# Six half units among a pair's head products, seven gathers per layer on the sync queue, and the first unit's sums two steps sooner

## The chip, the cores and the metric

One core of one Trainium2 chip runs the program. The time is device microseconds of one execution; where a profile is shown it is one execution taken by the hardware profiler. Engines: PE does the matmuls, DVE the elementwise work on two operands, ACT the activations and copies, POOL a few small operations, SP only issues DMAs. POOL and ACT can issue DMAs too; each issuing engine has a queue of its own.

## The reference

A trunk of two layers over 256 tokens of width 2048, all in float32:

```
h = rms_norm(x)
q, k, v, uv, gate_logits = split(h @ w_in)        # 1024 + 256 + 256 + 2048 + 4096 columns
a = attention(rope(rms_norm(q)), rope(rms_norm(k)), v, sinks) @ w_attn_branch   # window 128, 16 heads of 64
b = (u * (tril(w_spatial) v_norm + b_spatial)) @ w_sgu_branch                   # uv through gelu; u and v its halves
x = x + (sigmoid(gates)[:2048] * a + sigmoid(gates)[2048:] * b) @ w_out
h2 = rms_norm(x)
x = x + (silu(h2 @ w_gate) * (h2 @ w_up)) @ w_down                             # 5632 columns
```

## The kernel before

**Tiles.** The 256 tokens are two tiles of 128 rows and stay on the chip (xs). All weights are streamed once. The piece they come in is called a *half unit* here: 256 rows by 512 columns of a weight, 512 KB, one DMA on SP's queue (L193). Each piece is split in two: ACT rounds it to a short format (whi, L216) and DVE takes the rest (wlo, L217). The activations are split likewise (uh, ul, a *unit* being 512 of their columns, transposed). Every product is then hi·hi + hi·lo + lo·hi, the three matmuls of L303 to L305, 128x512 each. A half unit is 12 of them.

**Pairs and heads.** Two neighbouring chunks of 512 weight columns, such as two chunks of gates or the gate and up columns of the feed-forward part, make a *pair*. For the first unit of a pair the products are made by a Strassen-like scheme with seven products in place of eight. Six of them, P1, P5, P2, P6, P7, P4, of six matmuls each, make the *head* of the pair; the seventh, P3, and the other half units (tags G and U; X for a chunk without a partner) are its *body*. The scheme needs sums of weights (L204 on DVE) and sums of activations (sums, and their split sh and sl, L446), and it moves partial results while products run:

- after P5, which writes bank a[0], ACT copies a[0] to `kept` (L326) and a[1] to a[0] (L327); P2 goes on in a[0];
- after P6 and after P7 DVE adds a[1] to `kept` (L329); P7 and P4 go on in a[1];
- later the b banks are opened from `kept` (L332).

Each of these must be done before the next product in that bank. So the head is not run in one piece: half units of the plan before are put among its products. There are 49 heads among 1043 entries of the stream.

**Order.** PE's order is written out (the list `entries`). The order of the other engines is set by a scheduler at build time from the data they wait for. Loads are asked for 7 entries ahead, splits 4 ahead (four wsp buffers, so a split waits until PE is done with the one four before), sums 6 ahead. The raw pieces have five buffers, and the four pieces of a head (k11, k12, k21, k22) one each. The smaller work is hung on steps: `after(n, fn)` runs fn n steps later, a step (`tick`) being about one half unit.

**Turning a unit.** Before an activation can be a left operand it is transposed: DVE turns 32x32 blocks into one box (L373, one buffer), and 16 DMAs of 32 KB (L378) gather the box's blocks into tt (or kT for the keys). ACT then makes qT (L695) for the queries, or uh and ul. All gathers are issued by POOL, in order with its small operations, such as rq (L276), the factors of the normalisation of q (L650).

Of the kernel before, what the change touches and what calls it, by code (L numbers as in the profile page):

```python
# [30 lines left out]
B = 32  # L31
W_LOAD = 7
ROUNDS = ((0, 4), (4, 8), (8, 11))
WINO = 0
WINO_NORM = 7, 8, 10, 11, 12, 13
WINO_IN = 6, 7, 8, 12, 13, 14
WINO_MIX = 6, 7, 9, 10, 11, 13
WINO_HID = 7, 8, 17, 18, 19, 20
# [18 lines left out]
def hybrid_trunk(ctx: ExitStack, tc: tile.TileContext, x, mix_norm, w_in, q_norm, k_norm, sinks,  # L57
# [114 lines left out]
    for p in plans:  # L172
        if p.head:
            t = [entries.pop() for _ in range(5)][::-1]
            h = p.head
            entries += [t[0], h[0], t[1], h[1], t[2], h[2], h[3], t[3], h[4], t[4], h[5]]
        entries += p.body

    class Stream:
# [86 lines left out]
    first_cols = const.tile([P, 16], F32, name="first_cols")  # L266
    nc.vector.tensor_copy(first_cols, pf[:, :16])
    neg_half = const.tile([P, 24], F32, name="neg_half")
    nc.gpsimd.memset(neg_half, -0.5)
# [95 lines left out]

    def turn(dst, src):


        box = turned.tile([P, 4, 4, NT, B], F32, tag="box", name=nm("box"))
        iv = src.rearrange("p t (k j c) -> p t k j c", j=4, c=B)  # L370

        def blocks(t):
            nc.vector.transpose(box[:, :, :, t, :].rearrange("p j k r -> p k j r"), iv[:, t])  # L373

        def gather():
            for j in range(4):
                for i in range(4):
                    nc.gpsimd.dma_start(dst[j * B:(j + 1) * B, i], box[i * B:(i + 1) * B, j])  # L378

        blocks(0)  # L380
        after(1, lambda: (blocks(1), gather()))

    def transposed(units, c, src, cols=None, on_pe=False, wino=None, again=False):

# [34 lines left out]
        tt = slot([P, 4, 4, NT, B], name="tt")  # L419
        turn(tt, src)  # L420

# [50 lines left out]
    class Norm:  # L472
# [13 lines left out]
        def unit(self, c, on_pe=False, again=False):  # L486
            transposed(self.units, c, xs[:, :, c * CW:(c + 1) * CW], cols=self.cols[:, 4 * c:4 * c + 4],
                       on_pe=on_pe, again=again,
                       wino=None if c != WINO or on_pe else WINO_IN if self.soon else WINO_NORM)

# [25 lines left out]
    after(7, lambda: norm.finish())  # L516
    after(12, lambda: norm.unit(WINO, again=True))

# [106 lines left out]
    class Attention:  # L625
# [46 lines left out]
        def keys(self, kv):  # L672
            self.kv = kv
            kd = slot([P, NT, NKV, 2, HD], name="kd")
            self.rotate(kv[:, :, :KVW], NKV, self.pl.rope[1], [kd[:, :, :, j, :] for j in range(2)])
            self.kT = slot([P, 4, NKV, NT, B], name="kT")
            after(K_TURN, lambda: turn(self.kT, kd.rearrange("p t n a d -> p t (n a d)")))

        def queries(self, c, q):
            self.rotate(q, NQ // 2, self.pl.rope[0], None)  # L680
            self.qT[c] = slot([P, 4, S], name="qT")
            self.att[c] = slot([P, NT, CW], name="att")
            after(Q_TURN, lambda: self.turn_queries(c, q))
            n = Q_FIRST + (4 * Q_STEP - 8) * c
            for t in range(NT):
                for g in (2 * c, 2 * c + 1):
                    after(n, lambda t=t, g=g: self.scores(t, g))
                    n += Q_STEP
            after(n + 6, lambda: transposed(self.attT, c, self.att[c]))

        def turn_queries(self, c, q):
# [5 lines left out]

            turn(tt, q)
            after(5, lambda: ordered(0))
# [57 lines left out]
    class Spatial:  # L757
# [49 lines left out]
        def u(self, c, ps):  # L807
# [3 lines left out]
            for b in range(2):  # L811
                after(12 + 3 * b, lambda b=b: self.mix(c, b, ut))
            after(18 + 6 * c, lambda: transposed(self.sguT, c, ut))

# [171 lines left out]
```

## Time and profile before

| | |
|---|---|
| median of 3 runs | 2518.38 us (2517.23 to 2518.81) |
| the profiled execution | 2517.02 us |
| its span, first to last instruction | 2515.3 us |
| mean granted clock of PE | 0.994 |
| PE busy | 2477.4 us, 98% |
| DVE busy | 1942.2 us, 77% |
| ACT busy | 1443.6 us, 57% |
| POOL busy | 390.9 us, 16% |
| read from memory | 475.27 MB, 190 GB/s over the span |

The profile is to be read from PE: the idle time of another engine costs nothing unless PE waits for it. In a line of the profile the time stands first, then the engine, the line of the program, the operation and the tiles; brackets name the wait before it and what ended it. The granted clock is the share of full speed that PE was given in a stretch.

### The profile page before, as it was taken

How to read it: one execution, taken by the hardware profiler on the slowest of the kernel's cores; microseconds unless marked ns; L12 is line 12 of the kernel's file. 1: busy time of each engine (PE TensorE's matmuls, PEld its weight loads, DVE VectorE, ACT ScalarE, POOL GpSimd, SP SyncE). 2: the span in 40 equal slices, each digit the busy share in tenths (PEclk: the TensorE clock that was granted, in tenths of full speed). 3: DMA queues.
4: the chain of work that ended last, by engine and by line, in shares of the span. 5: the costliest groups of instructions: out<-in, count | busy, mean ns of one | idle time of the engine just before them, and what ended most of it. 6: DMA issues, size and time to landing. Idle time of an engine off the chain costs nothing. (4 is left out here: it accounts for less than half of the span.)

```text
span 2515.3 us, 31287 instructions
## 1 busy us (share of the span) xinstructions
PE 2477.4 (98%) x11076; PEld 2035.7 (81%) x11076; DVE 1942.2 (77%) x2279; ACT 1443.6 (57%) x1808; POOL 390.9 (16%) x751
## 2 busy tenths in 40 slices
PE   9899999999999999999999999999999999999999
PEld 7678888788888888888887788887888888888887
DVE  6788766688877778777888986767878777877786
ACT  5566545566655565455666665445756555655564
POOL 3401212131110011002114012122311101110110
PEclk9999999999999999999999999999999999999999
DMA  8555657567575666566667556675766666665754
GB/s 294 172 158 177 194 176 236 188 193 232 179 234 175 220 199 220 182 208 211 209 181 237 153 158 211 201 216 172 229 194 219 199 201 204 208 208 186 223 185 151
DMA packets 272078, 502.54 MB, mean 200 GB/s; under 512 B 26224, under 2 KB 28880, under 8 KB 271920
## 3 DMA queue, kind: packets, MB, share of 16 engines
q1 hardware_dynamic: 248720, 476.90, 60.1%
q0 software_dynamic: 22880, 23.37, 3.1%
q8 instruction: 87, 1.43, 0.2%
q14 instruction: 71, 0.58, 0.1%
q10 hardware_dynamic: 320, 0.27, 0.0%
HBM read 475.27 MB, written 2.10 MB: 190 GB/s over the span
## 5 line engine op out<-in xcount | busy, mean ns | idle before, releaser
L217 DVE TENSOR_TENSOR wlo<-raw,whi 128x1024 fp32r<-128x1024 f32 (+1 forms) x1045 | 1271.4, 1219 | 528.3 <-ACT whi L216 519.2
L216 ACT ACTIVATE whi<-raw 128x1024 fp32r<-128x1024 f32 (+1 forms) x1045 | 1104.0, 1058 | 973.5 <-PE acc L305 823.7
L303 PE MATMUL acc<-whi,uh 128*128 128x512 f32 x3094 | 1213.4, 392 | 16.1 <-ACT acc L327 10.2
L304 PE MATMUL acc<-wlo,uh 128*128 128x512 f32 x3094 | 1207.5, 390 | 2.3 <-DVE wlo L217 2.3
L305 PE MATMUL acc<-whi,ul 128*128 128x512 f32 x3094 | 1207.3, 390 | 0.0
L303 PEld LDWEIGHTS acc<-whi,uh 128*128 128x128 f32 x3094 | 582.6, 188 | 140.3 <-ACT acc L327 12.6
L304 PEld LDWEIGHTS acc<-wlo,uh 128*128 128x128 f32 x3094 | 582.8, 188 | 124.1 <-DVE wlo L217 4.8
L305 PEld LDWEIGHTS acc<-whi,ul 128*128 128x128 f32 x3094 | 582.5, 188 | 122.7 <-DVE ul L405 0.2
L378 POOL DMA_DIRECT2D tt<-box x672 | 329.7, 498 | 1727.8 <-DVE box L373 655.9
L204 DVE TENSOR_TENSOR raw<-raw,raw 128x1024 f32<-128x1024 f32 x196 | 238.9, 1219 | 0.5
L303 PE MATMUL acc<-whi,sh 128*128 128x512 f32 x392 | 158.8, 405 | 5.9 <-DVE kept L329 5.8
L305 PE MATMUL acc<-whi,sl 128*128 128x512 f32 x392 | 154.4, 394 | 4.3 <-DVE sl L446 4.3
L304 PE MATMUL acc<-wlo,sh 128*128 128x512 f32 x392 | 154.3, 394 | 0.0
L303 PEld LDWEIGHTS acc<-whi,sh 128*128 128x128 f32 x392 | 74.5, 190 | 32.9 <-issue 12.4
L305 PEld LDWEIGHTS acc<-whi,sl 128*128 128x128 f32 x392 | 74.7, 191 | 20.7 <-DVE sl L446 4.7
L304 PEld LDWEIGHTS acc<-wlo,sh 128*128 128x128 f32 x392 | 74.7, 190 | 14.0
L329 DVE TENSOR_TENSOR kept<-acc,kept 128x512 f32<-128x512 f32 x98 | 66.8, 682 | 3.9 <-PE acc L305 3.9
L332 ACT ACTIVATE acc<-kept 128x512 f32<-128x512 f32 x98 | 56.4, 587 | 6.4 <-DVE kept L329 6.3
L837 DVE SCALAR_TENSOR_TENSOR xs<-acc,xs 128x512 f32<-128x512 f32 (+1 forms) x66 | 42.6, 667 | 7.8 <-PE acc L305 7.8
L925 ACT ACTIVATE hid<-acc,rhalf 128x512 f32<-128x512 f32 x44 | 30.4, 690 | 19.2 <-PE acc L305 19.1
L326 ACT ACTIVATE kept<-acc 128x512 f32<-128x512 f32 x49 | 29.3, 597 | 15.1 <-PE acc L305 15.1
L728 ACT ACTIVATE pr<-pr,negm 128x128 f32<-128x128 f32 (+1 forms) x64 | 28.2, 443 | 7.8 <-DVE negm L721 7.7
(136 smaller groups left out, 899.9 us busy)
## 6 DMA issues: line engine op xcount, KB each, us to landing
raw<-in_w_in_dram SPq DMA_DIRECT2D x239, 512.0 KB, 4.4
raw<-in_w_up_dram SPq DMA_DIRECT2D x176, 512.0 KB, 4.7
raw<-in_w_gate_dram SPq DMA_DIRECT2D x176, 512.0 KB, 4.6
raw<-in_w_down_dram SPq DMA_DIRECT2D x176, 512.0 KB, 4.8
raw<-in_w_out_dram SPq DMA_DIRECT2D x64, 512.0 KB, 4.7
tt<-box POOLq DMA_DIRECT2D x672, 32.0 KB, 4.2
raw<-in_w_attn_branch_dram SPq DMA_DIRECT2D x32, 512.0 KB, 4.5
raw<-in_w_sgu_branch_dram SPq DMA_DIRECT2D x32, 512.0 KB, 4.2
```

Of the source, the lines that this page charges most:

```text
L204: self.last = nc.vector.tensor_tensor(out=self.raws[d], in0=self.raws[x], in1=self.raws[y], op=ALU.subtract)
L216: nc.scalar.activation(hi[:, i, :], raw[:, i, :], AF.Copy)
L217: self.last = nc.vector.tensor_tensor(out=lo[:, i, :], in0=raw[:, i, :], in1=hi[:, i, :].bitcast(F32), op=ALU.subtract)
L303: nc.tensor.matmul(ps, a, hi[:, kk, :], start=first and kk == 0, stop=False, skip_group_check=True)
L304: nc.tensor.matmul(ps, a, lo[:, kk, :], start=False, stop=False, skip_group_check=True)
L305: nc.tensor.matmul(ps, b, hi[:, kk, :], start=False, stop=kk == 1, skip_group_check=True)
L326: nc.scalar.activation(p.kept[:, 1, :], a[0], AF.Copy)
L329: nc.vector.tensor_tensor(out=p.kept[:, int(tag == "P7"), :], in0=a[1], in1=p.kept[:, 1, :], op=ALU.add)
L332: nc.scalar.activation(ps, p.kept[:, t, :], AF.Copy)
L378: nc.gpsimd.dma_start(dst[j * B:(j + 1) * B, i], box[i * B:(i + 1) * B, j])
L837: nc.vector.scalar_tensor_tensor(out=xs[:, t, sl], in0=sums[t][:, i * w:(i + 1) * w], scalar=scale, in1=xs[:, t, sl], op0=ALU.mult, op1=AL ...
L925: nc.scalar.activation(th, g[t], AF.Tanh, scale=norm.rh[t])
```

## The change

Four edits.

1. **Order of a head.** Before, five half units of the plan ahead stand around and among the head's products: t0 P1 t1 P5 t2 P2 P6 t3 P7 t4 P4. Now it is n, the smaller of six and the number of entries in that plan's body. With six: t0 P1 t1 P5 t2 t3 P2 P6 t4 P7 t5 P4. With four, where the plan ahead is a chunk of a branch product with four half units: t0 P1 t1 P5 P2 P6 t2 P7 t3, and P4 comes after the first entry of the pair's own body. 45 heads get six, four get four: in each layer the pair of gate chunks 5 and 6 and the first pair of the output projection (mix).
2. **Queue.** `turn` takes the queue of the gather. The gathers of kT, of the two chunks of q, of the two of the attention's result and of the two of the gating unit go to SP, 7 per layer, 14 in all and 224 DMAs. The other 30 stay on POOL.
3. **First unit's sums.** For the first unit of layer 0, made a second time from a gather (`again`), the steps are 6 to 11 in place of 7, 8 and 10 to 13.
4. **Its start.** That gather is hung on step 10 in place of 12.

```diff
@@ -34,6 +34,7 @@
 WINO = 0
 WINO_NORM = 7, 8, 10, 11, 12, 13
 WINO_IN = 6, 7, 8, 12, 13, 14
+WINO_FIRST = 6, 7, 8, 9, 10, 11
 WINO_MIX = 6, 7, 9, 10, 11, 13
 WINO_HID = 7, 8, 17, 18, 19, 20
 W_SPLIT = 4
@@ -171,10 +172,15 @@
     entries = []
     for p in plans:
         if p.head:
-            t = [entries.pop() for _ in range(5)][::-1]
-            h = p.head
-            entries += [t[0], h[0], t[1], h[1], t[2], h[2], h[3], t[3], h[4], t[4], h[5]]
+            h, n = p.head, min(6, len(ahead.body))
+            t = [entries.pop() for _ in range(n)][::-1]
+            entries += [t[0], h[0], t[1], h[1]] + t[2:n - 2] + [h[2], h[3], t[n - 2], h[4], t[n - 1]]
+            if n == 6:
+                entries.append(h[5])
+            else:
+                p.body.insert(1, h[5])
         entries += p.body
+        ahead = p
     class Stream:
@@ -265,6 +271,7 @@
     nc.tensor.transpose(pf[:, :16], first_rows, ident[:16, :16])
     first_cols = const.tile([P, 16], F32, name="first_cols")
     nc.vector.tensor_copy(first_cols, pf[:, :16])
+
     neg_half = const.tile([P, 24], F32, name="neg_half")
     nc.gpsimd.memset(neg_half, -0.5)
@@ -363,7 +370,7 @@
         while p.left:
             step()
-    def turn(dst, src):
+    def turn(dst, src, queue):
         box = turned.tile([P, 4, 4, NT, B], F32, tag="box", name=nm("box"))
@@ -375,12 +382,12 @@
         def gather():
             for j in range(4):
                 for i in range(4):
-                    nc.gpsimd.dma_start(dst[j * B:(j + 1) * B, i], box[i * B:(i + 1) * B, j])
+                    queue.dma_start(dst[j * B:(j + 1) * B, i], box[i * B:(i + 1) * B, j])
         blocks(0)
         after(1, lambda: (blocks(1), gather()))
-    def transposed(units, c, src, cols=None, on_pe=False, wino=None, again=False):
+    def transposed(units, c, src, cols=None, on_pe=False, wino=None, again=False, queue=None):
@@ -417,7 +424,7 @@
             return
         tt = slot([P, 4, 4, NT, B], name="tt")
-        turn(tt, src)
+        turn(tt, src, queue or nc.gpsimd)
         def blocks_of(k0):
             return lambda k, step: tt[:, :, k0 + k:k0 + k + step].rearrange("p i k t r -> p (k t) i r")
@@ -486,7 +493,8 @@
         def unit(self, c, on_pe=False, again=False):
             transposed(self.units, c, xs[:, :, c * CW:(c + 1) * CW], cols=self.cols[:, 4 * c:4 * c + 4],
                        on_pe=on_pe, again=again,
-                       wino=None if c != WINO or on_pe else WINO_IN if self.soon else WINO_NORM)
+                       wino=None if c != WINO or on_pe else WINO_FIRST if again else WINO_IN if self.soon else
+                       WINO_NORM)
         def finish(self):
             self.r, self.rh, self.rr = [], [], []
@@ -514,7 +522,7 @@
     for c in range(NCH):
         after(3 + c, lambda c=c: norm.squares(c))
     after(7, lambda: norm.finish())
-    after(12, lambda: norm.unit(WINO, again=True))
+    after(10, lambda: norm.unit(WINO, again=True))
     mask = const.tile([P, S], F32, name="mask")
     nc.gpsimd.memset(mask, 0.0)
@@ -674,7 +682,7 @@
             kd = slot([P, NT, NKV, 2, HD], name="kd")
             self.rotate(kv[:, :, :KVW], NKV, self.pl.rope[1], [kd[:, :, :, j, :] for j in range(2)])
             self.kT = slot([P, 4, NKV, NT, B], name="kT")
-            after(K_TURN, lambda: turn(self.kT, kd.rearrange("p t n a d -> p t (n a d)")))
+            after(K_TURN, lambda: turn(self.kT, kd.rearrange("p t n a d -> p t (n a d)"), nc.sync))
         def queries(self, c, q):
             self.rotate(q, NQ // 2, self.pl.rope[0], None)
@@ -686,7 +694,7 @@
                 for g in (2 * c, 2 * c + 1):
                     after(n, lambda t=t, g=g: self.scores(t, g))
                     n += Q_STEP
-            after(n + 6, lambda: transposed(self.attT, c, self.att[c]))
+            after(n + 6, lambda: transposed(self.attT, c, self.att[c], queue=nc.sync))
         def turn_queries(self, c, q):
             tt = slot([P, 4, 4, NT, B], name="tt")
@@ -695,7 +703,7 @@
                 nc.scalar.activation(self.qT[c][:, k:k + 2].rearrange("p k (t i r) -> p (k t) i r", t=NT, r=B),
                                      tt[:, :, k:k + 2].rearrange("p i k t r -> p (k t) i r"), AF.Copy)
-            turn(tt, q)
+            turn(tt, q, nc.sync)
             after(5, lambda: ordered(0))
             after(6, lambda: ordered(2))
@@ -810,7 +818,7 @@
                 after(1 + t, lambda t=t: self.gelu(ut, t))
             for b in range(2):
                 after(12 + 3 * b, lambda b=b: self.mix(c, b, ut))
-            after(18 + 6 * c, lambda: transposed(self.sguT, c, ut))
+            after(18 + 6 * c, lambda: transposed(self.sguT, c, ut, queue=nc.sync))
         def mix(self, c, b, ut):
             pg = ps_at.tile([P, 2, NT, P], F32, tag="at", name=nm("psg"))
```

What the edits do to the rows of ACT at the pair of gate chunks 5 and 6 in layer 0, before. whi_3224 is the split for P5, 3246 for t2, 3259 for P2, 3279 for P6, 3293 for t3, 3311 for P7:

```order
L216 ACTIVATE whi_3224<-raw_3127 128x1024
L216 ACTIVATE whi_3246<-raw_3185 128x1024
L216 ACTIVATE whi_3259<-raw_3204 128x1024
L216 ACTIVATE whi_3279<-raw_3127 128x1024
L326 ACTIVATE kept_3290<-acc_3251 128x512
L216 ACTIVATE whi_3293<-raw_3244 128x1024
L327 ACTIVATE acc_3251<-acc_3252 128x512
L216 ACTIVATE whi_3311<-raw_3129 128x1024
L216 ACTIVATE whi_3324<-raw_3277 128x1024
```

The same place now; whi_3246 is for P5, 3265 for P2, 3279 for P6, 3298 for t2, 3311 for P7. The lines are some six to eight further down in the changed file (L216 is L222, L326 is L333, L327 is L334):

```order
L222 ACTIVATE whi_3246<-raw_3145 128x1024
L222 ACTIVATE whi_3265<-raw_3203 128x1024
L222 ACTIVATE whi_3279<-raw_3145 128x1024
L222 ACTIVATE whi_3298<-raw_3244 128x1024
L333 ACTIVATE kept_3308<-acc_3269 128x512
L222 ACTIVATE whi_3311<-raw_3147 128x1024
L334 ACTIVATE acc_3269<-acc_3270 128x512
```

The copies L326 and L327, which wait for P5, had a split between them and half unit t2 stood between P5 and P2 on PE; the split between them is there now too, and P2 is the product next to P5.

ACT at the first head of layer 1, before (qT is the transposed first chunk of q; whi_11236 is the split for P2, 11256 for P6, 11270 for t3, 11289 for P7):

```order
L216 ACTIVATE whi_11236<-raw_11181 128x1024
L216 ACTIVATE whi_11256<-raw_11079 128x1024
L216 ACTIVATE whi_11270<-raw_11220 128x1024
L216 ACTIVATE whi_11289<-raw_11081 128x1024
L695 ACTIVATE qT_10994<-tt_11127 128x512
L326 ACTIVATE kept_11267<-acc_11227 128x512
L695 ACTIVATE qT_10994<-tt_11127 128x512
L327 ACTIVATE acc_11227<-acc_11228 128x512
```

And now (whi_11236 is the split for P2, 11251 for P6, 11270 for t4, 11289 for P7):

```order
L222 ACTIVATE whi_11236<-raw_11181 128x1024
L333 ACTIVATE kept_11246<-acc_11206 128x512
L334 ACTIVATE acc_11206<-acc_11207 128x512
L222 ACTIVATE whi_11251<-raw_11060 128x1024
L222 ACTIVATE whi_11270<-raw_11216 128x1024
L222 ACTIVATE whi_11289<-raw_11062 128x1024
L703 ACTIVATE qT_10994<-tt_11128 128x512 x2
L222 ACTIVATE whi_11305<-raw_11249 128x1024
```

The two copies have moved from behind qT to three splits ahead of it.

SP in the first head of layer 0 now; tt_833 is the gather of the first chunk of q, which stood on POOL:

```order
L199 DMA raw_978<-in_w_in_dram 128x2x512
L199 DMA raw_1012<-in_w_in_dram 128x2x512
L199 DMA raw_1091<-in_w_in_dram 128x2x512
L385 DMA tt_833<-box_834 32x256 x16
L199 DMA raw_1104<-in_w_in_dram 128x2x512
L199 DMA raw_1117<-in_w_in_dram 128x2x512
L199 DMA raw_1146<-in_w_in_dram 128x2x512
```

The 16 DMAs of a gather stand among the loads of the half units and are issued when the box is turned, with the loads behind them.

## The prediction

> **What bounds the kernel now.** I read the page's totals first, then PE's list of waits, then the stretches around the waits with the busy time of every engine, then single instructions there. The lines of the page for the engines, and PE's waits (engine, line, what it waited for: us in total, times, longest):
>
> ```profile
> PE 2477.4 (98%) x11076; PEld 2035.7 (81%) x11076; DVE 1942.2 (77%) x2279; ACT 1443.6 (57%) x1808; POOL 390.9 (16%) x751
> ...
> PE acc L303 <- ACT acc L327: 10.2, 7, 4.5
> PE acc L303 <- DVE kept L329: 6.8, 10, 2.6
> PE acc L305 <- DVE sl L446: 4.3, 1, 4.3
> PE psc L711 <- ACT qT L695: 3.6, 1, 3.6
> PE acc L303 <- ACT gate L869: 2.7, 1, 2.7
> PE acc L304 <- DVE wlo L217: 2.3, 5, 0.6
> PE acc L303 <- ACT q L869: 1.8, 1, 1.8
> ```
>
> PE bounds it: of the 2515.3 us span 2477.4 are busy and only about 34 us are waits that these rows name. No matmul is removed, so nothing but these waits, and the clock behind them, can be won. The rows are a map: L327 (the copy that P2 needs), L329 (the sum that P7 and P4 need), sl (the first unit's sums) and qT are what the edits touch; the gate drain is not touched.
>
> The stretches in which they lie (us, then busy time of PE, PEld, DVE, ACT, POOL, then the granted clock):
>
> ```profile
> core 0: us, PE busy (x) PEld busy (x) DVE busy (x) ACT busy (x) POOL busy (x), PEclk, DMA share, GB/s
> 89.90:119.70 29.80, 19.61 (x71) 14.67 (x69) 26.77 (x34) 14.32 (x24) 11.01 (x18) 0.83 0.35 100
> 468.70:477.50 8.80, 4.31 (x13) 3.01 (x13) 4.98 (x6) 5.38 (x8) 0.00 (x0) 0.82 0.53 179
> 1354.50:1368.10 13.60, 9.98 (x41) 7.19 (x39) 13.12 (x15) 6.96 (x9) 2.89 (x2) 0.87 0.51 158
> 168.00:181.00 13.00, 10.42 (x41) 8.73 (x40) 12.05 (x28) 5.31 (x13) 1.00 (x1) 0.74 0.71 203
> ```
>
> These are the first head of layer 0, the first mix pair, the first head of layer 1 and the second head of layer 0. In three of the four it is DVE that is nearly full (26.77 of 29.80, 13.12 of 13.60, 12.05 of 13.00): there PE waits for a backlog, and a wait removed at one product may return at the next. The mix pair is another kind: ACT and DVE are half idle, a single chain on ACT is late.
>
> What a wait costs beyond itself shows in PE's instructions behind it (start, length, in brackets the wait before it):
>
> ```profile
> 473.62 0.50 PE L303 MATMUL acc<-whi,uh 128*128 128x512 f32 x1 [4.49 <-ACT acc L327]
> ...
> 474.51 0.63 PE L303 MATMUL acc<-whi,uh 128*128 128x512 f32 x1
> 474.93 0.63 PE L304 MATMUL acc<-wlo,uh 128*128 128x512 f32 x1
> ...
> 172.91 0.47 PE L303 MATMUL acc<-whi,sh 128*128 128x512 f32 x1 [2.58 <-DVE kept L329]
> ...
> 92.06 0.50 PE L303 MATMUL acc<-whi,uh 128*128 128x512 f32 x1 [1.77 <-ACT q L869]
> 92.40 0.39 PE L304 MATMUL acc<-wlo,uh 128*128 128x512 f32 x1
> 92.63 0.39 PE L305 MATMUL acc<-whi,ul 128*128 128x512 f32 x1
> ```
>
> Starts are 0.23 us apart at full clock (92.40 to 92.63) and 0.42 after the long idle (474.51 to 474.93). The matmuls behind the 2.58 and the 4.49 us waits ran so for six or seven instructions, some 1.3 us lost; those behind the 1.77 us wait did not. Restarting costs about 0.3 us besides (0.34 in place of 0.23 to the second matmul, and the overlap of some 0.16 lost). So a wait of w costs w + 0.3, and w + 1.6 once it is long.
>
> **The change part by part.** The profiled execution took 2517.02 us; the median of the three runs is 2518.38, 1.36 higher. I sum differences and take them off the median.
>
> *First unit's sums earlier, q's gather off POOL (first head).* Three of the rows above stand here: q 1.8, sl 4.3, qT 3.6. The stretch of 29.80 us holds 10.2 us of PE idle; with some 16 slow matmuls (3.2) and four restarts (1.2) that is 14.5 us lost. DVE and POOL there:
>
> ```profile
> 89.89 1.22 DVE L650 TENSOR_TENSOR q<-q,rq 128x1024 f32<-128x1024 f32 x1
> 95.06 1.23 DVE L661 TENSOR_TENSOR q<-q,ca 128x1024 f32<-128x1024 f32 x1
> 97.58 1.30 DVE L373 STREAM_TRANSPOSE box<-q 128x512 f32<-128x512 f32 x2
> 99.91 1.21 DVE L446 TENSOR_TENSOR sl<-sums,sh 128x1024 fp32r<-128x1024 f32 x1
> 122.13 0.66 DVE L329 TENSOR_TENSOR kept<-acc,kept 128x512 f32<-128x512 f32 x1
> ...
> 71.36 3.93 POOL L378 DMA_DIRECT2D kT<-box  x8
> 82.81 2.93 POOL L276 TENSOR_TENSOR rq<-ssq,neg_half 128x16 f32<-128x16 f32 x1
> ```
>
> POOL gathered kT from 71.36 to 82.8, and rq, which the rotation of q needs, came behind it. So the rotation sat on DVE at 89.89 to 97.5, just where sl and the head's sums fall due; sl came at 99.91 and P5 stood 4.28 us. With kT's gather on SP, rq is ready before 83, and the rotation lies in the half units before the head, where DVE still had gaps. In the new order sl also stands directly behind P1's split, two splits ahead of P5's. The DVE list from q's product to P7's sum (89.89 to 122.79, 33 us, 3 of them idle) loses the rotation (four operations, 5.0), sl (1.2), and, now behind the sum of P6 or P7, one operation and the two transposes of the next q (2.4): 8.6 less. P7's sum ends near 114 in place of 122.8. What stays late: qT by about 1.3 (its gather still follows the rotation), P2 by about 1.6 (the order puts P7's split ahead of its copy), P7 by about 2.6. With restarts that is some 7 of the 14.5: gain **7.5**. If DVE stays as full as now only the sl wait less a returned wait is won: 2. If P7 does not wait: 12.
>
> *Six half units (45 heads).* The copy that P2 needs has one half unit more. In the first head of layer 1 it is behind qT today:
>
> ```profile
> 1356.31 0.63 ACT L695 ACTIVATE qT<-tt 128x512 f32<-128x512 f32 x1 [0.27 <-DMA tt<-box]
> ...
> 1357.84 0.59 ACT L327 ACTIVATE acc<-acc 128x512 f32<-128x512 f32 x1
> ...
> 1358.48 0.80 PE L303 MATMUL acc<-whi,uh 128*128 128x512 f32 x1 [3.59 <-ACT acc L327]
> ```
>
> The new order has both copies three splits ahead of qT. The wait of 3.59 and 1.6 behind it are 5.2; DVE is full at 13.12 of 13.60, so I give 1.5 back at the sums: gain **3.7** (2 to 5.2). In the second head the 2.58 us wait for L329 costs 4.2 with its clock; the sum waits for a backlog of 12.05 in 13.00, and P7 comes one half unit (2.7 us) later: gain **3.6** (1 to 4.2). The small ones, L327 (five waits, 2.1 together) and L329 (nine, 4.2 together): the extra half unit hides the copies wholly, the sums only partly, since P7 still follows P6 by one half unit: **3.0** (0.7 to 4). The other heads never waited, and win nothing.
>
> *Four half units (the pair of gate chunks 5 and 6, the first mix pair; both layers).* Here the plan before has four half units only, and by the new order no half unit stands between P5 and P2. What P2 then waits for is visible at the second head, where the same three instructions follow P5's end:
>
> ```profile
> 160.07 0.60 ACT L326 ACTIVATE kept<-acc 128x512 f32<-128x512 f32 x1 [0.25 <-PE acc L305]
> 160.57 1.05 ACT L216 ACTIVATE whi<-raw 128x1024 fp32r<-128x1024 f32 x1
> 161.52 0.59 ACT L327 ACTIVATE acc<-acc 128x512 f32<-128x512 f32 x1
> ```
>
> From 160.07 to 162.11, with the signal 2.1 to 2.2 us, and today a half unit of 2.7 us covers it. That cover is gone. Queued behind the copy on ACT are only the splits of the next half units, four ahead of PE. Price: 2.15, restart 0.3, and the slow clock, which 1.77 did not bring and 2.58 did; I take half of 1.6: **3.3** each, bounds 2.1 and 4.1. Three of the four heads pay it whole, the one before layer 1's mix pair perhaps 0.6 more, since its P1 bank is drained by two gate activations. In layer 0's mix pair the 4.5 us wait is already there, and the same chain (a split, uh, two gate drains, two copies) starts from P5's end instead: 0. Sum **−10.5** (−6.9 to −13).
>
> [...]
>
> *Gathers on SP.* Seven gathers per layer, 14 in all, of 16 DMAs of 32 KB. Nothing is copied more or less; the queue that weights come through is held.
>
> ```profile
> L217 DVE TENSOR_TENSOR wlo<-raw,whi 128x1024 fp32r<-128x1024 f32 (+1 forms) x1045 | 1271.4, 1219 | 528.3 <-ACT whi L216 519.2
> L216 ACT ACTIVATE whi<-raw 128x1024 fp32r<-128x1024 f32 (+1 forms) x1045 | 1104.0, 1058 | 973.5 <-PE acc L305 823.7
> L378 POOL DMA_DIRECT2D tt<-box x672 | 329.7, 498 | 1727.8 <-DVE box L373 655.9
> ...
> L193 SPq DMA_DIRECT2D raw<-in_w_in_dram x239: 367/368/753, 3.6 to 1683.2; - x120
> ...
> raw<-in_w_in_dram SPq DMA_DIRECT2D x239, 512.0 KB, 4.4
> ...
> tt<-box POOLq DMA_DIRECT2D x672, 32.0 KB, 4.2
> ```
>
> At 0.367 us an issue 16 take 5.9 us; if the ninth waits for the first to land (on POOL kT's gather was broken so, 11.4 us with its gaps), 8.8 to 11.4. Cover: five buffers freed every 2.72 us, less a split of 1.2 and a landing of 4.4, leave 8 us until a split is late, and the splits run four ahead, 3 × 2.72 − 1.06 − 1.22 = 5.9 until PE is. 13.9 in all, more than 11.4: cost **0**. Without that cover each gather costs its excess.
>
> Sum: 7.5 + 3.7 + 3.6 + 3.0 − 10.5 = 7.3 gained. **2518.4 − 7.3 = 2511.1.**
>
> **The rivals.** *Fuller gains.* The clock keeps full speed at 2.15 us, and P7 no longer waits in the first two heads: the first head gains 12, the next two 5.2 and 4.2, the small ones 3, and the four heads cost 8: 16.4 gained at most, 13.9 with the first head at 9.5: 2504.5. For it: the 1.77 us wait. Against: DVE's shares above.
>
> *DVE takes the gains back.* The window rows say DVE bounds three of the four stretches, and no DVE instruction is removed there but only moved a few half units. First head 2 to 3, first head of layer 1 2, second head 1, small ones 2, together 7 to 8, against 8 to 10.5 paid at the four heads: no change, 2520 (2516 to 2522).
>
> *Slower: SP is held.* One gather holds SP past 13.9 us when it waits for its box's second transpose and then lands as slowly as kT's on POOL; the loads behind it come late, and PE waits for whi. At 16 us each 14 gathers would cost 14 × 2 = 28, less 7: 2539. It decides from 13.9 us on. Against: the order puts the loads next to each gather five to ten half units ahead of their splits.
> [...]
>
> *It doesn't do what it says*: the new order is not six half units at the four heads, as counted above.
>
> **How the numbers follow.** Forecast 0.46, fuller gains 0.20, DVE takes it back 0.24, slower 0.10. A difference under 0.2% (5.0 us) cannot be told from none. The forecast's own range is 2506.5 to 2515.5; its slower end, about a fifth of its chance, lies inside the 0.2%. Faster: 0.37 + 0.20 = 0.57; same: 0.24 + 0.09 = 0.33; slower 0.10. The range takes in the fuller gains down to 2503.5 and the third case up to 2520.
>
> **What would show it.** Right: PE's wait for sl gone; the L327 row with four waits of 2.1 to 4.5 us, all at heads with P2 directly behind P5, and about 1.6 at the first head; the L329 row near 3 to 5 us; P5 without a wait at the first head and the wait for qT near 1.3; no wait of PE or ACT for raw; PE busy shorter by the slow matmuls. Wrong: PE waits for whi or wlo behind a gather, a wait for qT as long as before, or L329 waits as large as the L327 waits that went.

## The result

The changed kernel takes 2503.10 us (median of 4 runs, 2502.16 to 2503.58), the kernel before 2517.81 (4 runs, 2515.98 to 2518.81). The ratio is 0.9942, 95% interval 0.9925 to 0.9959: 14.7 us faster. Forecast was 2511.1, 7.3 less, with a range that ended at 2503.5. The direction was right, the gain twice as large, and the time lies outside the range by 0.4 us, near the rival of fuller gains (2504.5). One execution in the whole record, of bare49_long below, took 4319.45 us at a mean granted clock of 0.553; no number here uses it.

The page of the changed kernel, the line of the engines, and PE's list of waits, with the same columns as before. L310 is the former L303, L311 is L304, L334 is L327, L336 is L329, L877 is L869, L703 is L695, L719 is L711:

```profile
PE 2470.9 (99%) x11076; PEld 2030.7 (81%) x11076; DVE 1950.7 (78%) x2279; ACT 1441.6 (58%) x1808; POOL 288.3 (12%) x527
...
PE acc L310 <- ACT acc L334: 12.2, 5, 4.5
PE acc L310 <- ACT gate L877: 4.0, 1, 4.0
PE acc L310 <- DVE mv L801: 1.7, 1, 1.7
...
PE psc L719 <- ACT qT L703: 1.7, 1, 1.7
PE acc L311 <- DVE wlo L223: 1.6, 3, 0.8
...
PE acc L310 <- DVE kept L336: 0.7, 1, 0.7
```

Two readings. The row for the copy (L334) has grown from 10.2 to 12.2 us, although 45 heads were given more room: five waits are left, three of 2.12, one of 4.5 and one of 1.3 at the first head. The row for DVE's sum fell from ten waits and 6.8 us to one of 0.7, and the rows for sl and for q's drain are gone.

The table sums, at each place, the time between the starts of neighbouring matmuls above 0.227 us, their median in the traces of before and after. It holds the wait, the restart and the slow clock, and so can be added up.

| place | before | after | gained | forecast |
|---|---|---|---|---|
| first head of layer 0 | 14.4 | 5.9 | 8.4 | 7.5 |
| second head | 4.9 | 2.3 | 2.7 | 3.6 |
| first head of layer 1 | 5.9 | 1.0 | 4.9 | 3.7 |
| 11 small waits of 0.2 to 0.5 us at other heads | 7.7 | 0 | 7.7 | 3.0 |
| the four heads with four half units, and the gate wait beside the last | 12.2 | 21.2 | −9.1 | −10.5 |
| all else | 17.2 | 18.6 | −1.4 | 0 |
| sum | 62.2 | 49.0 | 13.2 | 7.3 |

The span went from 2515.3 to 2500.5, by 14.8; the sum leaves out the time between the small matmuls of the attention and the transposes.

### The profile page after: what moved, and what is told of

Same layout as the page of the kernel before. It is cut to its first block, busy times and chain, and to the rows that moved or that the text cites. A ratio compares the mean times of both kernels' runs of the same rounds, so it can differ in the third digit from the quotient of the medians.

```text
span 2500.5 us, 31319 instructions
## 1 busy us (share of the span) xinstructions
PE 2470.9 (99%) x11076; PEld 2030.7 (81%) x11076; DVE 1950.7 (78%) x2279; ACT 1441.6 (58%) x1808; POOL 288.3 (12%) x527
## 5 line engine op out<-in xcount | busy, mean ns | idle before, releaser
L222 ACT ACTIVATE whi<-raw 128x1024 fp32r<-128x1024 f32 (+1 forms) x1045 | 1103.6, 1058 | 955.0 <-PE acc L312 767.7
L310 PE MATMUL acc<-whi,uh 128*128 128x512 f32 x3094 | 1213.0, 392 | 18.6 <-ACT acc L334 12.2
L311 PE MATMUL acc<-wlo,uh 128*128 128x512 f32 x3094 | 1207.4, 390 | 1.2 <-DVE wlo L223 0.8
L310 PEld LDWEIGHTS acc<-whi,uh 128*128 128x128 f32 x3094 | 582.3, 188 | 141.7 <-ACT acc L334 14.1
L311 PEld LDWEIGHTS acc<-wlo,uh 128*128 128x128 f32 x3094 | 582.5, 188 | 124.2 <-DVE wlo L223 4.4
L385 POOL DMA_DIRECT2D tt<-box x480 | 236.1, 499 | 1732.9 <-DVE box L380 608.2
L310 PE MATMUL acc<-whi,sh 128*128 128x512 f32 x392 | 158.0, 403 | 2.3 <-DVE mv L801 1.7
L311 PE MATMUL acc<-wlo,sh 128*128 128x512 f32 x392 | 153.6, 392 | 0.8 <-DVE wlo L223 0.8
L310 PEld LDWEIGHTS acc<-whi,sh 128*128 128x128 f32 x392 | 74.0, 189 | 29.3 <-issue 10.7
L311 PEld LDWEIGHTS acc<-wlo,sh 128*128 128x128 f32 x392 | 74.1, 189 | 14.8 <-DVE wlo L223 1.1
L336 DVE TENSOR_TENSOR kept<-acc,kept 128x512 f32<-128x512 f32 x98 | 66.9, 683 | 0.5 <-PE acc L312 0.5
L934 DVE SCALAR_TENSOR_TENSOR hid<-hid,acc 128x512 f32<-128x512 f32 x44 | 29.8, 684 | 9.3 <-ACT hid L933 9.3
L333 ACT ACTIVATE kept<-acc 128x512 f32<-128x512 f32 x49 | 29.2, 595 | 13.2 <-PE acc L312 13.2
```

The costliest lines, as they stand in the source:

```text
L222: nc.scalar.activation(hi[:, i, :], raw[:, i, :], AF.Copy)
L310: nc.tensor.matmul(ps, a, hi[:, kk, :], start=first and kk == 0, stop=False, skip_group_check=True)
L311: nc.tensor.matmul(ps, a, lo[:, kk, :], start=False, stop=False, skip_group_check=True)
L336: nc.vector.tensor_tensor(out=p.kept[:, int(tag == "P7"), :], in0=a[1], in1=p.kept[:, 1, :], op=ALU.add)
L385: queue.dma_start(dst[j * B:(j + 1) * B, i], box[i * B:(i + 1) * B, j])
L934: nc.vector.scalar_tensor_tensor(out=th, in0=th, scalar=1.0, in1=g[t], op0=ALU.add, op1=ALU.mult)
```

## Experiments

"Lost" below is the sum that the table uses, for one place. The experiments ran on three chips, which ran the kernel before in 2515.3 to 2515.8 us (medians), so they are compared by their ratios to it.

**five_at_four.** The four heads get the old order back, with the fifth half unit from the plan further ahead:

```diff
-            h, n = p.head, min(6, len(ahead.body))
+            h, n = p.head, 6 if len(ahead.body) >= 6 else 5
```

(with P4 always behind the last of them).

> The change, with the old order of five half units at the four heads whose plan ahead has four. Theory A (the four heads cost what the profile of the change shows there: two new waits of 2.12 us at P2 worth 2.7 each, and at the mix pair of layer 1 9.4 in place of 5.8, 9.1 in all; the rest of the change is independent of them): the waits of 2.12 us go, the gate wait is 2.7 again, and the time is 2503.1 - 9.1 = 2494. Rival B (the new order there pays by itself, since P4 behind G2 frees the last half unit, and what I read as price is the drain of the gates, late in any order): 2501 to 2504. By the price in the prediction (10.5): 2492.6.

Measured 2492.94 us, ratio 0.9912 (0.9898 to 0.9927). The change's own ratio is 0.9942, so the four heads cost about 0.3%, 7.5 us; by the spans, 2500.5 and 2493.5, 7.0. The three waits of 2.12 us are gone, and at the mix pair of layer 1 2.8 are lost in place of 9.4. The price was real, as theory A has it. It came out smaller than 9.1, since a wait that theory A did not know appeared at 299 us:

```profile
289.12 1.06 ACT L218 ACTIVATE whi<-raw 128x1024 fp32r<-128x1024 f32 x1 [2.58 <-DMA tt<-box]
...
297.04 1.16 ACT L399 ACTIVATE uh<-tt 128x512 fp32r<-128x512 f32 x2 [5.87 <-DMA tt<-box]
...
299.61 1.06 ACT L218 ACTIVATE whi<-raw 128x1024 fp32r<-128x1024 f32 x1 [0.84 <-DMA raw<-in_w_in_dram]
300.96 1.06 ACT L218 ACTIVATE whi<-raw 128x1024 fp32r<-128x1024 f32 x1 [0.30 <-DMA raw<-in_w_in_dram]
302.23 1.06 ACT L218 ACTIVATE whi<-raw 128x1024 fp32r<-128x1024 f32 x1 [0.21 <-DMA raw<-in_w_in_dram]
...
275.71 3.71 SPq L195 DMA_DIRECT2D raw<-in_w_in_dram  x7
279.52 16.10 SPq L381 DMA_DIRECT2D tt<-box  x16
295.72 1.55 SPq L195 DMA_DIRECT2D raw<-in_w_in_dram  x3
```

These are ACT's and SP's instructions (start, length). The second gather of the gating unit holds SP for 16.1 us, the loads behind it go out at 295.7, and the splits wait for raw. PE stood 0.75 us for whi and 0.77 for wlo.

**six_alone.** Only the order of the 45 heads, on the kernel before.

```diff
-            t = [entries.pop() for _ in range(5)][::-1]
+            n = 6 if len(ahead.body) >= 6 else 5
+            t = [entries.pop() for _ in range(n)][::-1]
```

> The kernel before with six half units at 45 heads and the old five at the other four; gathers on POOL and the first unit's sums as before. Theory A (the extra half unit alone removes the waits at the small heads, 6.9, at the first head of layer 1, 4.9, and at the second head of layer 0, 2.7): 14.5 less than before plus what P2's share of the first head gives, so 2502 to 2504. Rival (the two heads among queries and keys gained because the gathers left POOL): only the small heads, 2517.8 - 6.9 = 2511.

Measured 2501.99, ratio 0.9952 (0.9935 to 0.9968): 12 us less by the ratio, 13.5 by the medians. (The expectation took the small waits at 6.9 us; counted over all of them they are 7.7.) All eleven small waits are gone, so the rival is false; the second head loses 2.3 (4.9 before), the first head of layer 1 2.2 (5.9). The first head of layer 0 loses 14.6, as before. So the order explains, without the queue, all the gain but that of the first head.

**queue_sums, sums_alone, queue_alone.** The kernel before with the gathers on SP and the earlier sums, with the sums alone (`after(10, ...)` and WINO_FIRST), and with the queue alone (`queue.dma_start` with nc.sync for the 14 gathers).

> The kernel before with the gathers on SP and the first unit's sums two steps sooner, the order of the heads as before. Theory A: the first head of layer 0 gains its 8.4 by these two and nothing else moves, 2517.8 - 8.4 = 2509.4; the wait for sl is gone, that of 3.6 at the first head of layer 1 and the 4.5 at the first mix pair stay. Rival (the first head's gain needs the half unit between P5 and P2 too): 3 to 5 less than before, 2513 to 2515. Rival (holding SP costs): slower than 2517.8, with waits of PE for whi.

> The kernel before with only the first unit's sums two steps sooner. If the late sl is late because its step is late: its wait of 4.28 us goes, with its clock some 6 us, 2512, and the wait for qT stays 3.6 or grows. If it is late because DVE is full there (the rotation of q sits at the same place, since rq waits for POOL): the wait moves to the next product, and the time is within 2 us of before, 2516 to 2518.

> The kernel before with only the 14 gathers on SP. sums_alone won 2.3 and the two together 5.4 by medians (11 in their profiles). Theory (the rotation of q, early since rq no longer stands behind kT's gather, is what empties DVE there): first head 14.4 to about 7, 5 to 8 less than before, ratio 0.9975. Rival (sl is late by its step, whatever DVE does): the wait of 4.3 for sl stays, 2 to 3 less than before, 0.999.

| | median | ratio | lost at the first head | waits of PE there |
|---|---|---|---|---|
| sums_alone | 2513.17 | 0.9992 (0.9983 to 1.0001) | 11.7 | q 1.8, qT 5.9 |
| queue_alone | 2513.21 | 0.9991 (0.9981 to 1.0000) | 9.3 | q 1.8, qT 2.6, one more of 1.0 |
| queue_sums | 2510.04 | 0.9976 (0.9966 to 0.9986) | 4.4 | qT 1.4, P2's copy 1.8, P7's sum 0.9 |

(The kernel before loses 14.4 there.) The earlier step alone takes away the wait for sl, and the wait for qT grows from 3.6 to 5.9: DVE is as full as it was, and the wait has moved to the next product, as its second branch has it (2.0 less by the ratio). The queue alone takes away the same wait for sl, though its step is late: its rival expected 4.3 to stay, and it falls. How, DVE's instructions in queue_alone show:

```profile
80.14 1.23 DVE L653 TENSOR_TENSOR q<-q,rq 128x1024 f32<-128x1024 f32 x1 [0.42 <-POOL rq L278]
...
96.36 1.22 DVE L448 TENSOR_TENSOR sl<-sums,sh 128x1024 fp32r<-128x1024 f32 x1
```

The product of q with rq starts at 80.14 and not at 89.89, and sl comes at 96.36 and not at 99.91. That is the step of the prediction on rq behind kT's gather. With both, the first head's gain is there without the extra half unit, so the rival that needs it is false by the profile: 10 us less are lost at that place. By the medians the two give 5.4 (3.5 to 8.6 by the interval); the profiled execution, 2506.1, is the fastest of nine that reach to 2512.5. queue_alone gains less than its theory says: 5.1 at the first head in place of 7, of which the first head of layer 1 takes 1.4 back (7.3 lost, 5.9 before).

**sgu_pool and kt_only.** five_at_four with the gating unit's gathers back on POOL, and with all but kT's back.

```diff
-            after(18 + 6 * c, lambda: transposed(self.sguT, c, ut, queue=nc.sync))
+            after(18 + 6 * c, lambda: transposed(self.sguT, c, ut))
```

> five_at_four with the gathers of the gating unit (4 of the 14) back on POOL. In five_at_four SP was held for 16.1 and 15.3 us by the second of two such gathers, beyond the 13.9 us of cover, and PE waited for whi and wlo there (0.75 and 0.77 us at 300, 0.75 at 1542, 4.7 us with the clock behind them). If those waits are the loads held behind the gather, they go and the time is 3 to 4.5 less than five_at_four, a ratio to before of about 0.9896; if they come from elsewhere, nothing changes (0.9912).

> sgu_pool with the gathers of q and of the attention's result back on POOL too: only kT's gather is on SP. Theory A (the queue matters at the first head only because rq stood behind kT's gather on POOL): the first head costs some 5.5 as in five_at_four, ratio to before about 0.9896 as in sgu_pool. Rival (what helps is that the gathers from SP land in 1.9 us and not 4.2): the wait for qT grows by 2 to 3 us in the first head and the queries of layer 1 get one; 3 to 5 us slower than sgu_pool, about 0.991.

sgu_pool took 2496.75, ratio 0.9924 (0.9912 to 0.9936): no gain. The waits for held loads did go, as expected, but the gate wait at the mix pair of layer 1 rose from 2.5 to 5.9 us. ACT there, then POOL's issues of the gather that uh waits for; in the second block the same issues in five_at_four:

```profile
1685.55 1.06 ACT L218 ACTIVATE whi<-raw 128x1024 fp32r<-128x1024 f32 x1 [0.31 <-PE acc L308]
1690.94 1.15 ACT L399 ACTIVATE uh<-tt 128x512 fp32r<-128x512 f32 x2 [4.33 <-DMA tt<-box]
1692.00 1.24 ACT L873 ACTIVATE gate<-acc,rhalf 128x512 f32<-128x512 f32 x2
...
1677.33 3.42 POOL L381 DMA_DIRECT2D tt<-box  x7 [10.09 <-ACT whi L218]
1683.31 4.40 POOL L381 DMA_DIRECT2D tt<-box  x9 [2.56 <-issue]
```

```profile
1681.65 7.81 POOL L381 DMA_DIRECT2D tt<-box  x16 [9.70 <-ACT whi L218]
```

The gate drain that frees PE's bank stands behind uh, and uh waits for its gather. That gather is on POOL in all kernels. In sgu_pool its 16 issues were broken by a pause of 2.56 us and took 10.4 us in place of 7.8, which is most of the 3.4 us by which the wait grew. What makes POOL pause is not shown.

kt_only took 2507.84, ratio 0.9967 (0.9955 to 0.9979), 11 us slower than sgu_pool. Theory A (only kT's gather matters) is false: with q's gathers on POOL the first head loses 8.8 in place of 5.8, the first head of layer 1 3.8 in place of 1.2, and some 4.4 more go in the two stretches behind it. That is more than twice what the rival expected, and its cause, the landing, explains a small part only. In the page's table of DMAs one DMA of a gather lands in 4.2 us (median; 4.1 in kt_only) when POOL issues it and in 1.9 when SP does, but SP takes longer to issue the 16: for the first chunk of q 10.0 us in sgu_pool, where POOL took 7.9 in kt_only. From the end of the second transposition to the last landing the gather of the first chunk of q takes 11.3 us in sgu_pool and 11.5 in kt_only; in layer 1 11.9 and 14.1, with a pause among POOL's issues there:

```profile
1332.59 3.49 POOL L381 DMA_DIRECT2D tt<-box  x7 [1.08 <-PE acc L308]
1338.56 4.55 POOL L381 DMA_DIRECT2D tt<-box  x9 [2.48 <-issue]
```

What else differs is the order of ACT. In sgu_pool qT starts within 0.2 us of the landing. In kt_only it stands behind splits and starts 1.2 us after it at the first head and 3.7 us after it in layer 1 (landed 1346.13, started 1349.85). So moving the gathers changed the order that the scheduler made, and the 11 us are not the price of the queue alone; how they part was not tested.

**late_unit and late_unit_pool.** In five_at_four and sgu_pool, the unit of the third chunk for the mix pair is made four steps later, so that its uh does not stand ahead of the gate drain and the two copies on ACT.

```diff
-            after(6, lambda: parts(0, 2, blocks_of(0)))
-            after(7, done)
+            after(at[0], lambda: parts(0, 2, blocks_of(0)))
+            after(at[1], done)
...
+                                                                   at=(10, 11) if j in (2,) else (6, 7)))
```

> five_at_four, with the unit of the third chunk for the mix pair (uh, ul) made four steps later. Theory: the 4.5 us wait at the first mix pair (before, after and in every kernel so far) and the gate wait at layer 1's are one thing: on ACT the gate drain and the two copies stand behind that unit's uh, which waits for its gather. Both waits go (7.3 and 2.8 us with their clock): 10 less than five_at_four, a ratio to before of 0.987. Rival (the copies wait for a buffer or for P5 as such): the wait stays between 2 and 4.5, ratio 0.990 to 0.991.

> late_unit with the gating unit's gathers back on POOL. In sgu_pool this removed the waits for held loads (3.7 and 1.0) and the gate wait grew from 2.5 to 5.9 with a slow clock, because uh waited longer for its gather with the drain behind it. With the drain no longer behind uh the first remains and the second is gone: 4 to 4.7 less than late_unit, ratio 0.985. If moving those gathers costs by itself (POOL is held for others), no gain over late_unit.

late_unit took 2483.11, ratio 0.9874 (0.9859 to 0.9889), where 0.987 was expected. late_unit_pool took 2482.33, ratio 0.9871 (0.9854 to 0.9887): 33 us less than the kernel before and about 18 less than the change. Between the two no difference can be told; 4 to 4.7 was expected, and late_unit lost only 2.4 at the held loads, with no slow clock there. The ACT rows at the first mix pair, in the change and in late_unit_pool:

```profile
460.86 1.06 ACT L222 ACTIVATE whi<-raw 128x1024 fp32r<-128x1024 f32 x1 [0.30 <-PE acc L312]
461.82 1.13 ACT L403 ACTIVATE uh<-tt 128x512 fp32r<-128x512 f32 x2
462.86 1.25 ACT L877 ACTIVATE gate<-acc,rhalf 128x512 f32<-128x512 f32 x2
464.00 0.59 ACT L333 ACTIVATE kept<-acc 128x512 f32<-128x512 f32 x1
464.62 0.58 ACT L334 ACTIVATE acc<-acc 128x512 f32<-128x512 f32 x1
```

```profile
455.86 0.60 ACT L329 ACTIVATE kept<-acc 128x512 f32<-128x512 f32 x1 [0.23 <-PE acc L308]
456.36 1.05 ACT L218 ACTIVATE whi<-raw 128x1024 fp32r<-128x1024 f32 x1
457.31 0.59 ACT L330 ACTIVATE acc<-acc 128x512 f32<-128x512 f32 x1
```

The 4.5 us wait that stood in the kernel before and in the change was an order of ACT, not a need of the data: the copies now run right behind P5, and PE has no wait at either mix pair. In the change uh did not wait for its gather there (no bracket at 461.82), as the theory had it; the place of the drain and the copies behind it was enough. At layer 1 uh does wait for its gather: late_unit_pool has a pause of 2.5 us in that gather too, and PE has no wait behind it.

**bare49 and bare49_long.** The price of one wait, many times: P2 and P6 directly behind P5 in all 49 heads; then the copy to kept made twice.

```diff
+            entries += [t[0], h[0], t[1], h[1], h[2], h[3]] + t[2:n - 1] + [h[4], t[n - 1], h[5]]
```

> The change with P2 directly behind P5 and P6 behind P2 in all 49 heads, the half units that stood there moved behind P6: the price of one such wait, 49 times. If a wait of 2.1 us costs 2.7 (wait, restart, clock not slowed) as in the two heads of the change: 2503 + 45 x 2.7 = 2625. If it slows the clock every second time, as the prediction took it: 2655. If every time: 2688.

> bare49 with the copy of a[0] to kept made twice, which makes each of the 49 waits about 0.5 us longer, 2.6 us. If the length of the wait decides whether the clock is slowed, with its point between 2.1 and 2.6 (2.58 and 2.71 slowed it in the kernel before): 49 x (2.6 + 0.6 + 1.4), so 2503 + 45 x 4.6 = 2710. If the length doesn't decide (2.54 to 2.89 did not slow it at the same place in four other kernels): a share of the waits only, 2650 to 2680.

bare49 took 2635.64 (two runs, 2633.3 to 2638.0), bare49_long 2693.19 (one run). The first lies between no slowed clock (2625) and every second (2655), the second between a share of the waits (2650 to 2680) and all of them (2710): the wait slows the clock sometimes. In bare49 36 waits are of exactly 2.12 us; 25 cost 2.4 us (2.12 and a restart of 0.27) and 11 about 4.0, with 6 to 8 matmuls at half clock. In bare49_long 36 are of 2.73 us; 15 cost 3.0 and 21 about 4.6. Two waits of bare49:

```profile
793.45 0.50 PE L306 MATMUL acc<-whi,uh 128*128 128x512 f32 x1 [2.12 <-ACT acc L330]
793.78 0.39 PE L307 MATMUL acc<-wlo,uh 128*128 128x512 f32 x1
...
794.48 0.39 PE L307 MATMUL acc<-wlo,uh 128*128 128x512 f32 x1
794.71 0.40 PE L308 MATMUL acc<-whi,ul 128*128 128x512 f32 x1
```

```profile
746.32 0.50 PE L306 MATMUL acc<-whi,uh 128*128 128x512 f32 x1 [2.12 <-ACT acc L330]
...
747.58 0.54 PE L308 MATMUL acc<-whi,ul 128*128 128x512 f32 x1
747.92 0.63 PE L306 MATMUL acc<-whi,sh 128*128 128x512 f32 x1
748.35 0.63 PE L307 MATMUL acc<-wlo,sh 128*128 128x512 f32 x1
748.78 0.63 PE L308 MATMUL acc<-whi,sl 128*128 128x512 f32 x1
```

The same wait, and 1.3 us later the matmuls start 0.43 apart in the second and not in the first. So neither theory on the length is right as it stood.

## Why the prediction was wrong

**The step that failed** is the term for the small waits, under "Six half units": "the extra half unit hides the copies wholly, the sums only partly, since P7 still follows P6 by one half unit: 3.0". It measured 7.7, which is 4.7 of the 7.4 us by which the forecast was short; the other rows of the table together make 1.2, and 1.5 lie in what the table leaves out. Two errors in it. The waits were summed bare, without the restart of 0.3 that the prediction had itself worked out: the eleven are 4.5 us bare and 7.7 with it, so this is some 3.2 of the 4.7. And the sums' waits went altogether, the other 1.5; six_alone, which changes the order and nothing else, shows the same. (Three of the fourteen waits that the term counted lie elsewhere: 0.5 at the first head, 0.5 at 1409.9 that cost 0.1, and 0.7 at 1422.6 that stayed.) I looked at the distance from P6 to P7, which indeed did not change, and not at the list that DVE has ahead of the sum. DVE at a pair of the feed-forward part before, with PE's wait there, and at the same pair in the change:

```profile
777.67 1.22 DVE L204 TENSOR_TENSOR raw<-raw,raw 128x1024 f32<-128x1024 f32 x1
778.80 1.22 DVE L217 TENSOR_TENSOR wlo<-raw,whi 128x1024 fp32r<-128x1024 f32 x1
779.94 0.68 DVE L329 TENSOR_TENSOR kept<-acc,kept 128x512 f32<-128x512 f32 x1
...
780.76 0.47 PE L303 MATMUL acc<-whi,sh 128*128 128x512 f32 x1 [0.50 <-DVE kept L329]
```

```profile
766.96 1.23 DVE L223 TENSOR_TENSOR wlo<-raw,whi 128x1024 fp32r<-128x1024 f32 x1 [0.26 <-ACT whi L222]
768.10 1.22 DVE L210 TENSOR_TENSOR raw<-raw,raw 128x1024 f32<-128x1024 f32 x1
769.23 1.22 DVE L223 TENSOR_TENSOR wlo<-raw,whi 128x1024 fp32r<-128x1024 f32 x1
770.37 0.68 DVE L336 TENSOR_TENSOR kept<-acc,kept 128x512 f32<-128x512 f32 x1
```

Before, split, sum of weights and sum of products follow each other without a gap from 773 on. In the change DVE waits 0.26 us for a split shortly before: its list has run empty. A head product gives PE 1.36 us of work (six starts 0.227 apart) and DVE a whole split of 1.2, often with a sum of weights of 1.2; the half unit put in ahead of P2 gave DVE the time to pay that debt off. Five of the six waits of 0.5 us for a sum look like this one: no gap of DVE in the 8 us ahead of P6's sum before, and 0.26 in the change. At the sixth (1317.9) DVE has no gap in either, so why that wait went is not shown.

That the time came near the rival of fuller gains is luck. The first two heads of layer 0 gained less than it had (8.4 and 2.7, where it had 9.5 to 12 and 4.2), and the small waits, which it took at the same 3.0, made up for them. That rival's 8 for the four heads is three unslowed waits of 2.15 + 0.3 and the 0.6 of the fourth; 9.1 was measured.

**First head of layer 0**, forecast 7.5, measured 8.4: right in mechanism. queue_alone and sums_alone show that the queue emptied DVE and the early step did not. Left are qT 1.67 (1.3 forecast) and P2 1.33 (1.6 forecast); the wait of 2.6 at P7 did not come, and 12 slow matmuls did, and so did a wait of 0.8 for P5's split, where the prediction had P5 without one.

**The second head of layer 0 and the first of layer 1**, forecast 3.6 and 3.7, measured 2.7 and 4.9: inside their bounds. The second head's wait for L329 is gone, and one for the statistics of the gating unit (mv, 1.7) took a part of its place.

**The four heads**, forecast −10.5, measured −9.1 in the profile and about −7.5 by five_at_four, which has the held loads against it. The wait was read from three ACT instructions as 2.15 and is 2.12 in three places; the chain of 4.5 at layer 0's mix pair moved to P5 unchanged, as written. The sum added half of 1.6 for the clock on top of the restart, though by its own rule the 1.6 held the restart; by that rule a head costs 3.1 and not 3.3. In bare49 a slowed clock costs 1.6 on top of it, so the slip did no harm. The clock was costed at half chance and stayed up in all three:

```profile
363.56 0.50 PE L310 MATMUL acc<-whi,uh 128*128 128x512 f32 x1 [2.12 <-ACT acc L334]
363.89 0.39 PE L311 MATMUL acc<-wlo,uh 128*128 128x512 f32 x1
364.12 0.40 PE L312 MATMUL acc<-whi,ul 128*128 128x512 f32 x1
```

That all three stayed up is in part luck: at the share of bare49 (25 of 36) it happens one time in three. Nor did the lengths that the prediction went by, 1.77 us unslowed and 2.58 slowed, bound anything: the same wait of 1.77 us slowed seven matmuls in sums_alone. The gate wait before the last of them grew from 2.7 to 4.0 where 0.6 more was expected: the drain stood behind a uh that waited for its gather, whose 16 issues on POOL took 9.1 us in place of 7.8. The prediction did not see this.

**Gathers on SP at no cost** was right for the change, and closer than the prediction had it. Most held SP for 10.0 to 11.2 us (8.8 to 11.4 forecast), but the second of the gating unit's gathers 14.6 and 14.3, past the 13.9 of cover. Its sign "no wait of PE or ACT for raw" did not come: ACT's waits for loads of w_in and of the attention branch went from 6 with 5.2 us to 27 with 31.9. Almost none of it reached PE in the change, a wait of 0.13 us; in five_at_four, with SP held for 16.1 and 15.3 us, 4.7 us were lost. The rival "SP is held" has its point where it was put; it just was not far beyond it. The move changed more than POOL's time: in the change a DMA of a gather lands in 1.9 us from SP and in 4.2 from POOL (medians), though the whole gather wins little by it, as kt_only shows.

## What to carry to other kernels

Cost a wait with what follows it, and a wait for a backlogged engine by what that engine has in its list ahead of the instruction waited for: room given upstream, here a half unit two products ahead, can drain the list, so moving the consumer isn't the only cure. Where a new order is chosen by a rule, look at the cases in which the rule's material runs short (four half units in place of six); there the change gave back about a third of what it won, and undoing it there took two lines. A wait that stays the same in every variant is worth a question of its own: here an order on one engine that the data did not need cost some 10 us, two thirds of what the change won.

## What the runs showed of the hardware

Whether the clock was halved behind a wait was not decided by its length alone: of the 36 waits of 2.12 us in bare49 11 were slowed and 25 not. I took for each of them the start of the matmul behind it, and its remainder by a period. With a period of 3.413 us, and with no other between 1.5 and 8 (in steps of 0.0002), the slowed and the unslowed waits part into two unbroken arcs; the same period, found apart, does it for the 36 waits of 2.73 us in bare49_long:

```
remainder by 3.4133 us     not slowed          slowed
bare49, 2.12 us            0.35 to 1.99 (25)   2.20 to 3.41 and 0 to 0.31 (11)
bare49_long, 2.73 us       1.75 to 2.66 (15)   2.71 to 3.41 and 0 to 1.20 (21)
```

The trace's record of the granted clock shows the same directly. Around the second wait of bare49 above (us, then busy time of PE, PEld, DVE, ACT, POOL, then the granted clock):

```profile
744.26:747.67 3.41, 1.35 (x6) 1.13 (x7) 2.85 (x3) 2.01 (x3) 0.00 (x0) 1.00 0.31 86
747.67:751.08 3.41, 3.41 (x10) 2.63 (x9) 2.08 (x3) 1.41 (x2) 0.00 (x0) 0.50 0.61 221
751.09:754.50 3.41, 3.41 (x17) 2.81 (x16) 2.69 (x3) 1.97 (x3) 0.00 (x0) 1.00 0.60 160
```

One window holds nearly all of the wait (744.20 to 746.32), the next has half the clock, and the third the full clock again. In all 13 traces the stretches at half clock between the start and the end of the program are one to four times 3.413 us long, and within a trace they begin on one grid of that period, to 5 ns.

What is counted in these windows no trace records. A reading that fits is that PE's idle time adds up within one window, and that the next is at half clock when the sum is large enough. In the traces of before and after, behind the first 12 us, every window at full clock with 1.95 us of idle PE or more was followed by one at half clock, and none with 1.91 or less was: in the kernel before PE was busy for 1.46 of the 3.41 us from 95.44, and the next window had 0.50, and for 1.50 from 105.68, and the next had 1.00. When half clock ends the reading does not tell: at 173.94 in the kernel before a second window at 0.50 followed one in which PE is shown busy throughout.

The two arcs give an estimate of the same sum. The slowed arc is 1.5 to 1.8 us for the shorter and 1.9 to 2.5 for the longer wait. By the reading an idle time w puts at least c into one window of 3.413 if it starts within an arc of 3.413 + w − 2c. With w counted between matmul starts less the usual 0.23 (2.28 and 2.89), both arcs give c of about 2.0 us: an estimate from these two widths. It fits that the 1.77 us wait for q's drain (1.9 so counted, 2.0 with the restart) went both ways: it did not slow the clock in the kernel before, where a window ended 0.04 us before the wait did, and it did in sums_alone, where wait and restart lay in one window. It fits too that 1.67 and 1.33 us close together at the first head did so in the change, while 1.65 and 1.33 at the same place in five_at_four did not.

One consequence: in bare49 and bare49_long a wait of the same 2.12 or 2.73 us cost 1.6 us more or not (4.0 or 2.4, 4.6 or 3.0) by where the window happened to lie. The gate wait beside layer 1's mix pair slowed 13 matmuls at 2.71 us in the kernel before and none at 2.54 in five_at_four, 2.89 in six_alone and 2.59 in queue_sums. So a difference of 1.6 us between two of these profiles at such a wait says nothing of the edit.
